# Half-slab weight loads in prompt attention, six gate buffers in the attention output product, and another staging order in the first down product

## The chip, the cores and the metric

The kernel runs on one core of one Trainium2 chip. The metric is the device time of one execution in microseconds (us); the time of a kernel is the median of several such runs. In the profile PE is the matrix engine (PEld its weight loads), DVE the vector engine, ACT the scalar engine, POOL the general engine, and SP the engine that here only issues transfers. "SPq" is SP's queue: it issues its DMAs in order, and a DMA that waits for a semaphore holds up those behind it.

## What is computed

One inference step of a decoder layer over 544 tokens (512 of a prompt, 32 of eight samples), float32, width 1024:

```python
mod = silu(c) @ w_ada + b_ada                      # six vectors of 1024
h   = rmsnorm(x, norm1) * (1 + sc1) + sh1
bg, cg, xin, q, k.., v.., gates, merge = split(h @ w_in)
y_a = (bg * conv3(cg * xin)) @ w_out_conv          # short convolution branch
o_b = sparse_attention(q, k.., v.., gates)         # compressed + selected + window
ga, gb = sigmoid(merge)
x   = x + g1 * ((ga * y_a + gb * (o_b @ w_o_nsa)) @ w_out)
h2  = rmsnorm(x, norm2) * (1 + sc2) + sh2
x   = x + g2 * ((silu(h2 @ w_gate) * (h2 @ w_up)) @ w_down)
y   = rmsnorm(x, norm_f)
```

For the prompt, every query attends in 128-query blocks; for the samples, past rows come from a paged cache.

## The kernel before, in words

Activations stand feature-major, 128 features by 544 tokens, in eight chunks. A product in full precision is made of three matrix passes over a high and a low part of both operands (`mm3`, L252 to L254). The weights are packed on the host into slabs `wt` of up to 128 x 2048 floats (8 KB a partition). `slab(...)` (L235) takes one of three rotating buffers `raw` (L216) and starts one load on SP (L238); `split(...)` (L241) turns 128 output columns of a slab into `wh` on ACT (L247) and `wl` on DVE (L248), each with two buffers. The framework traces the program, orders the instructions of each engine once, when it is built, by priority in program order and by its own estimate of when each is ready, and adds the waits. Within an engine that order is then fixed: an instruction that waits holds all that stand behind it. `issue_after` adds an ordering edge on one engine, not a wait.

Three places matter here.

**Prompt attention** (L1345 to L1560). Sixteen units, for g = 0..3 and i = 3..0; they are numbered 0 to 15 below. A unit (`unit`, L1434) makes scores on PE (`sp`, L1448 to L1456), takes their minimum with the distance table on DVE (L1461), exponentiates on ACT (L1462), and in its second half transposes the probabilities on PE (`ptp`, L1489), copies them on ACT or DVE (L1403, L1405) and multiplies by the values (`acc`, L1483). Beside each unit the loop does one step of `oc_gen` (L1383), which is half of one of eight chunks of the convolution branch's output product (eight triples of matrix passes over `yin`, then a DVE multiply by a reloaded gate `ga`, L1395), and one `mod_slab` (L426), which multiplies the conditioning vectors by one `ada` slab straight out of `raw` (`modp`, L432; 32 short matmuls). So 16 `ada` slabs and four `oc` slabs, each of 1 MB and each `oc` slab holding two chunks, pass through the three `raw` buffers, in order of the requests. An `ada` buffer comes free with its `modp`, an `oc` buffer with the split of its second chunk. `presum` (L562) adds a DRAM-to-DRAM copy (`pre`, L573, on SP) and an accumulating one (L576, on POOL) for later stages. In units 0, 1, 4, 5, 8 and 9 the loop also reloads the queries and keys of the next g (L1360, L1367).

**The attention's output product** (L1562 to L1600). Eight chunks with `o` slabs; each result is multiplied by the sigmoid of a reloaded gate `gb` (L1592, L1593; two buffers), added to the convolution branch's result and split again. Ahead of it the whole residual input `x1` (2.1 MB) is requested (L1565).

**The first down product** (`down_plain`, L1855), which stands between the gate product and the up product of the third pair of the feed-forward network. Eight chunks are staged in six places, two each in `U`, `Gs[1]` and `dsp`, from which POOL adds them to `x1` in DRAM by an accumulating DMA (L1853). Chunks 6 and 7 use the first two places again. After it the up product's first results are added into `U` (L1838).

Of the kernel before, what the change touches and what calls it, by code (L numbers as in the profile page):

```python
# [20 lines left out]
KC = 8  # L21
# [74 lines left out]
def _slabs():  # L96

    r = np.arange(1024).reshape(8, 128)
    d = {}

    def add(key, src, rows, c0, n):
        d[key] = (src, rows, np.arange(c0, c0 + n))

    for v in range(2):
        d["phi", v] = ("w_phi1", np.arange(2048).reshape(16, 128) + 2048 * v, np.arange(128))
    for s in range(24):
        add(("ada", s), "w_ada", r, s * 256, 256)
    add(("gate",), "w_in", r, C_GATE, 128)

    def quarters(key, src, cols, rows=r):  # L110
        n = len(rows)
        d[key] = (src, np.concatenate([rows[:n // 2], rows, rows[n // 2:]]), np.concatenate([np.tile(cols[i], (n // 2, 1)) for i in (1, 0, 0, 1)]))

    for ty in range(3):
        for v in range(2):
            quarters(("kv", ty, v), "w_in", [C_KV + ty * 512 + v * 256 + m * 128 + np.arange(128) for m in range(2)])
    for gp in range(2):
        for rp in range(2):
            quarters(("q", gp, rp), "w_in", [np.concatenate([np.arange(64) + C_Q + (2 * gp + gg) * 256 + (2 * rp + r2) * 64 for gg in range(2)]) for r2 in range(2)])
    for k2 in range(4):  # L120
        for n, c in (("cg", C_CG), ("xin", C_XIN), ("bg", C_BG), ("ga", C_MERGE), ("gb", C_MERGE + 1024)):
            if n == "ga" or (n == "gb" and k2 < GB7) or (n in ("cg", "xin", "bg") and k2 >= CV7):
                quarters((n, k2), "w_in", [c + k2 * 256 + m * 128 + np.arange(128) for m in range(2)])
            else:
                add((n, k2), "w_in", r, c + k2 * 256, 256)
        add(("oc", k2), "w_out_conv", r, k2 * 256, 256)
        p = np.arange(128)
        j = np.arange(8)
        rows = (2 * (j[:, None] // 4) + p[None, :] // 64) * 256 + (j[:, None] % 4) * 64 + p[None, :] % 64
        add(("o", k2), "w_o_nsa", rows, k2 * 256, 256)  # L130
        add(("out", k2), "w_out", r, k2 * 256, 256)
        for ph, (c0, n) in enumerate(PHASES):
            r6 = np.arange(c0 * 128, (c0 + n) * 128).reshape(n, 128)
            if ph in (1, 2):
                quarters(("dn", ph, k2), "w_down", [k2 * 256 + m * 128 + np.arange(128) for m in range(2)], np.concatenate([r6[0::2], r6[1::2]]))
            else:
                add(("dn", ph, k2), "w_down", r6, k2 * 256, 256)
    for c2 in range(FC // 2):
        for n, w in (("fg", "w_gate"), ("fu", "w_up")):
            if c2 == 0:  # L140
                add((n, c2), w, r, 0, 256)
            else:
                quarters((n, c2), w, [c2 * 256 + m * 128 + np.arange(128) for m in range(2)])
    return d
# [12 lines left out]
def build(tc, a, o):  # L157
# [16 lines left out]
    def lin_ps(nm):  # L174
        return ps.tile([128, 512], F32, tag="g", bufs=5, name=nm)

    def tp_ps(nm):
        return ps.tile([128, 512], F32, tag="g", bufs=5, name=nm)
# [9 lines left out]
    def nm(s):  # L188
        uid[0] += 1
        return f"{s}_{uid[0]}"  # L190
# [44 lines left out]
    def slab(*key):  # L235
        nk, ncol = len(SLABS[key][1]), SLABS[key][2].shape[-1]
        v = raw_tile("raw")[:, 0:nk * ncol]
        last_slab[0] = queue(lambda: sync.dma_start(v, a["wt"][SLAB_AT[key], :, 0:nk * ncol]))  # L238
        return v.rearrange("p (k f) -> p k f", k=nk)

    def split(view, nk=8, perm=None):  # L241
        wh = wpool.tile([128, 8, 128], F32R, tag="wh", bufs=2, name=nm("wh"))
        wl = wpool.tile([128, 8, 128], F32R, tag="wl", bufs=2, name=nm("wl"))
        oh, ol = wh[:, 0:nk, :], wl[:, 0:nk, :]
        if perm is not None:
            oh, ol = perm(oh), perm(ol)
        act.activation(oh, view, AF.Copy)  # L247
        dve.tensor_sub(ol, view, oh.bitcast(F32))  # L248
        return wh[:, 0:nk, :], wl[:, 0:nk, :]
# [158 lines left out]
    def hcols(hf):  # L408
        return slice(*HS[hf])
# [13 lines left out]
    MODS = {4: (0,), 5: (1,), 6: (2,), 7: (3,), 8: (4, 5), 9: (6, 7)}  # L423
    AHEAD = {4: 3, 5: 4, 6: 5, 7: 6, 8: 7}

    def mod_slab(s, v=None):  # L426
        v = slab("ada", s) if v is None else v
        p = tp_ps(nm("modp"))
        for k in range(KC):
            for hh in range(2):  # L430
                j = (k % 2) * 2 + hh
                pe.matmul(p[32 * j:32 * j + 32, 0:128], lhsT=cT[:, k, :], rhs=v[:, k, hh * 128:(hh + 1) * 128], start=(k < 2), stop=(k >= 6))  # L432
        m4 = wpool.tile([128, 128], F32, tag="m4", bufs=2, name=nm("m4"))
        act.activation(m4, p[:, 0:128], AF.Copy)
        if modp:
            modp.pop()()
        modp.append(lambda: mod_fin(s, m4))
# [929 lines left out]
            sync.dma_start(t[n * 64:n * 64 + 64].rearrange("p r x -> p (r x)").bitcast(F32), q_dr[gp][n][me])  # L1367
        return t

    oc_slabs = [slab("oc", 0)]  # L1370
    qst, kst = q_stack(0), k_stack(0)
    for br in range(2):
        vload = sync.dma_start(vtok[br].rearrange("p i f -> p (i f)"), v_dr[br])
    with tc.issue_after(vload.ins):
        mods_ahead = [slab("ada", 8), slab("ada", 9)]
    yst = ExitStack()
    y3p = mkpool(yst, "y3p", side="right")
    yh, yl = (y3p.tile([128, KC, NT], F32R, name="yin_" + n_) for n_ in ("hi", "lo"))
# [2 lines left out]
    pc0 = at.tile([128, 4, 4, 32], F32, name="pc0")  # L1381

    def oc_gen():  # L1383
        for k2 in range(4):
            so = slab("oc", k2) if k2 else oc_slabs[0]
            for kk in range(2):
                k = k2 * 2 + kk
                wh, wl = split(so[:, :, kk * 128:(kk + 1) * 128])
                for hf in range(2):
                    t = ga_next.pop(0) if ga_next else ga_tile(hf)  # L1390
                    sync.dma_start(t, ga_dr[k][:, hcols(hf)])
                    p = lin_ps(nm("lin"))[:, 0:HW[hf]]
                    for kc in range(KC):
                        mm3(p, wh, wl, yh[:, kc, hcols(hf)], yl[:, kc, hcols(hf)], kc, kc == 0, kc == KC - 1)
                    dve.tensor_mul(C[:, k, hcols(hf)], p, t)  # L1395
                    yield

    pcnt, p_ops, e_ops = [0], [], []

# [131 lines left out]
    for g in range(4):  # L1531
        qs, ks = qst, kst
        pc = cmp_probs(g, qs) if g else first_pc
        for i in (3, 2, 1, 0):
            u = unit(g, i, ks, qs, pc) if g or i < 3 else first_unit
            if g or i < 3:
                next(u)
            next(ocf, None)
            mod_slab(nslab, mods_ahead.pop(0) if mods_ahead else None)
            nslab += 1  # L1540
            presum(g > 0 or i < 2)
            if prev is not None:
                next(prev, None)
            prev = u
            if g < 3 and i == 3:
                qst = q_stack(g + 1)
            if g < 3 and i == 2:
                kst = k_stack(g + 1)
# [13 lines left out]
    x1_slot = lambda n, dt, w=NT: x1p.tile([128, KC * NT // w, w], dt, tag="x1", bufs=1, name=n)  # L1562
    x1 = x1_slot("x1", F32)
    lo_slot = lambda n, dt: x1p.tile([128, KC, NT], dt, tag="lo", bufs=1, name=n)
    sync.dma_start(x1.rearrange("p k n -> p (k n)"), a["xT"])  # L1565
    n2st = ExitStack()
    n2 = mkpool(n2st, "n2")
    zst = ExitStack()
# [15 lines left out]
    for k2 in range(4):  # L1584
        sy = slab("o", k2)
        win_shift(k2 // 2, k2 % 2)
        presum()
        for kk in range(2):
            k = k2 * 2 + kk
            cs = slice(kk * 128, kk * 128 + 128)  # L1590
            gb = op5.tile([128, NT], F32, tag="gb", bufs=2, name=nm("gb"))
            sync.dma_start(gb, gb_dr[k])  # L1592
            act.activation(gb, gb, AF.Sigmoid)  # L1593

            def ev(hf, p):
                c = hcols(hf)
                dve.tensor_mul(gb[:, c], p, gb[:, c])
                dve.tensor_add(C[:, k, c], C[:, k, c], gb[:, c])
                to_hilo(C[:, k, c], zh[:, k, c], zl[:, k, c])
            linear(split(sy[:, :, cs]), (oh, ol), ev)  # L1600
# [254 lines left out]
    def down_plain():  # L1855

        nk = PHASES[0][1]
        stg = [t[:, m, :] for t in (U, Gs[1], dsp) for m in range(2)]
        for m in range(KC):
            if m % 2 == 0:  # L1860
                sl_ = slab("dn", 0, m // 2)
            w = split(sl_[:, :, (m % 2) * 128:(m % 2) * 128 + 128], nk=nk)
            t = stg[m % 6]
            for hf in range(2):
                p = lin_ps(nm("dn"))[:, 0:HW[hf]]
                for k in range(nk):
                    mm3(p, w[0], w[1], fh[k][:, hcols(hf)], fl[k][:, hcols(hf)], k, k == 0, k == nk - 1)
                gated(t, hcols(hf), p, m, g2m)
            add_x1(m, t)
# [246 lines left out]
```

## Time and profile before

| | us |
|---|---|
| median of 3 runs (lowest, highest) | 1189.29 (1188.83, 1190.13) |
| profiled execution, its own time | 1192.38 |
| its span in the profile | 1190.6 |
| PE busy | 1174.8 |
| DVE busy | 850.7 |
| ACT busy | 639.8 |
| POOL busy | 106.8 |

Busy time of PE is modelled from pipelined matmuls, so 99% of the span says that PE seldom stands still, not that it runs at its peak. What can be gained by moving transfers shows as idle time of PE and as time at a lower granted clock; both are found in tables of stretches. A chain of waits tells which instruction released which; a row of it is start, duration, and engine with line or transfer. In rows of instructions, a bracket at the end gives the idle time of that engine just before it and what ended it.

### The profile page before, as it was taken

Reading aid. Unit: us, or ns where it says so; the run is one execution under the profiler, and the core shown is the slowest. Engines: PE = TensorE matmul, PEld = TensorE weight load, DVE = VectorE, ACT = ScalarE, POOL = GpSimd, SP = SyncE. Lnnn points to the kernel's source line nnn. Section 1 sums busy time; section 2 is a strip of 40 time slices with the busy share of each in tenths; the row PEclk is TensorE's granted clock in tenths of the full one; section 3 lists DMA queues with packets and bytes.
Section 4 is the critical chain, followed back from the end, with each engine's and each line's share of the span. In section 5 each row is a group of like instructions: output and inputs, shape, how many; then the busy total and the mean of one; then the engine's idle time right before and its main releaser. Section 6 shows DMA issues by size and latency. Waiting matters only on the chain.

```text
span 1190.6 us, 25817 instructions
## 1 busy us (share of the span) xinstructions
PE 1174.8 (99%) x10098; PEld 1090.9 (92%) x10098; DVE 850.7 (71%) x1930; ACT 639.8 (54%) x1302; POOL 106.8 (9%) x157
## 2 busy tenths in 40 slices
PE   9999999999999999999999999999999999999997
PEld 6999999999999888887776779999999999999996
DVE  2539986788774676777776866758847887887776
ACT  1416644565555333486665765527646566666542
POOL 1000340000000111020101100000010001001000
PEclk9999999999999999999999999999999999999999
DMA  9964765888666998979886878544356359349412
GB/s 339 357 254 143 195 203 159 266 255 231 216 182 216 360 371 316 306 209 245 243 224 183 216 222 286 173 164 165 91 153 197 129 136 238 128 123 222 173 54 75
DMA packets 87643, 250.68 MB, mean 211 GB/s; under 512 B 9560, under 2 KB 20184, under 8 KB 76010
## 3 DMA queue, kind: packets, MB, share of 16 engines
q1 hardware_dynamic: 73890, 223.56, 54.1%
q0 software_dynamic: 12912, 24.17, 12.7%
q8 instruction: 79, 1.29, 0.4%
q10 hardware_dynamic: 720, 1.31, 0.3%
q14 instruction: 42, 0.34, 0.1%
HBM read 217.64 MB, written 66.33 MB: 239 GB/s over the span
## 4 chain that ended last, share of the span: by engine, by line
PE 83%; DVE 5%; DMA 5%; issue 5%; ACT 1%; POOL 0%; ACTq 0%; SPq 0%; POOLq 0%; DVEq 0%
PE wA L254 8%; PE wA L252 7%; PE wA L253 7%; PE lin L252 6%; PE lin L253 6%; PE lin L254 6%; PE phi L677 5%; PE wC L253 4%; PE wC L254 4%; PE wC L252 4%; PE acc L1483 3%; PE ptp L1489 3%; PE modp L432 2%; PE wB L252 2%; PE wB L253 2%
## 5 line engine op out<-in xcount | busy, mean ns | idle before, releaser
L412 ACT ACTIVATE Wh<-raw 128x512 fp32r<-128x512 f32 (+3 forms) x83 | 63.1, 760 | 50.2 <-PE wA L253 34.5
L413 DVE TENSOR_TENSOR Wl<-raw,Wh 128x512 fp32r<-128x512 f32 (+3 forms) x83 | 70.9, 855 | 22.9 <-ACT Wh L412 22.4
L301 ACT ACTIVATE work<-wA 128x272 f32<-128x272 f32 x102 | 39.9, 391 | 68.9 <-PE wA L254 67.1
L1462 ACT ACTIVATE P<-P,nms 128x384 f32<-128x384 f32 (+3 forms) x120 | 64.9, 543 | 20.1 <-DVE nms L1461 19.4
L1461 DVE CUSTOM_DVE_ANT_0 P<-sp,ta 128x384 f32<-128x384 f32 (+3 forms) x120 | 52.1, 469 | 30.0 <-PE sp L1449 22.6
L413 DVE TENSOR_TENSOR wl<-ws,wh 128x1024 fp32r<-128x1024 f32 (+1 forms) x50 | 59.5, 1189 | 16.8 <-ACT wh L412 15.3
L412 ACT ACTIVATE wh<-ws 128x1024 fp32r<-128x1024 f32 (+1 forms) x50 | 51.3, 1026 | 35.0 <-PE wC L253 23.3
L413 DVE TENSOR_TENSOR wl<-raw,wh 128x1024 fp32r<-128x1024 f32 (+2 forms) x56 | 64.7, 1155 | 4.5 <-ACT wh L412 4.2
L252 PE MATMUL lin<-h_h,wh 128*128 128x288 f32 (+1 forms) x224 | 66.9, 299 | 0.3 <-ACT pts L197 0.3
L253 PE MATMUL lin<-h_l,wh 128*128 128x288 f32 (+1 forms) x224 | 64.6, 289 | 0.0
L254 PE MATMUL lin<-h_h,wl 128*128 128x288 f32 (+1 forms) x224 | 64.5, 288 | 0.0
L677 PE MATMUL phi<-gt,wphi 128*128 128x128 f32 x512 | 61.4, 277 | 0.7 <-DMA gt<-in_cache_cmp 0.7
L412 ACT ACTIVATE wh<-raw 128x1024 fp32r<-128x1024 f32 (+2 forms) x56 | 55.9, 999 | 11.3 <-PE wB L253 4.9
L677 PEld LDWEIGHTS phi<-gt,wphi 128*128 128x128 f32 x512 | 59.1, 192 | 2.9 <-DMA gt<-in_cache_cmp 1.7
L248 DVE TENSOR_TENSOR wl<-raw,wh 128x1024 fp32r<-128x1024 f32 (+1 forms) x42 | 47.1, 1121 | 20.1 <-ACT wh L247 19.8
L247 ACT ACTIVATE wh<-raw 128x1024 fp32r<-128x1024 f32 (+1 forms) x42 | 40.9, 973 | 35.6 <-PE lin L253 25.0
L576 POOL DMA_DIRECT2D pre<-in_wt x29 | 28.4, 980 | 340.6 <-DMA pre<-in_wt 340.4
L252 PE MATMUL wA<-S_hi,Wh 128*128 128x272 f32 x184 | 53.5, 291 | 0.0
L254 PE MATMUL wA<-S_hi,Wl 128*128 128x272 f32 x184 | 53.1, 290 | 0.2 <-DVE Wl L413 0.2
L253 PE MATMUL wA<-S_lo,Wh 128*128 128x272 f32 x184 | 53.1, 288 | 0.0
L252 PEld LDWEIGHTS lin<-h_h,wh 128*128 128x128 f32 x224 | 42.2, 188 | 10.9 <-issue 10.3
L668 DVE TENSOR_TENSOR xs<-gt 128x1024 f32<-128x1024 f32 x16 | 19.5, 1222 | 36.3 <-PE phi L677 20.6
(592 smaller groups left out, 4392.6 us busy)
## 6 DMA issues: line engine op xcount, KB each, us to landing
raw<-in_wt SPq DMA_DIRECT2D x67, 1024.0 KB, 5.6
raw<-in_wt SPq DMA_DIRECT2D x25, 768.0 KB, 5.0
sraw<-in_cache_sel SPq DMA_DIRECT2D x64, 256.0 KB, 5.1
gt<-in_cache_cmp SPq DMA_DIRECT2D x60, 256.0 KB, 5.5
pre<-in_wt SPq DMA_DIRECT2D x21, 512.0 KB, 9.1
pre<-in_wt POOLq DMA_DIRECT2D x21, 512.0 KB, 7.3
wraw<-in_cache_winT SPq DMA_DIRECT2D x8, 1024.0 KB, 8.4
raw<-pre SPq DMA_DIRECT2D x21, 256.0 KB, 5.6
```

Source lines behind the costliest of these rows:

```text
L247: act.activation(oh, view, AF.Copy)
L248: dve.tensor_sub(ol, view, oh.bitcast(F32))
L252: pe.matmul(p, lhsT=wh[:, k, :], rhs=xh, start=start, stop=False, **kw)
L253: pe.matmul(p, lhsT=wh[:, k, :], rhs=xl, start=False, stop=False, **kw)
L254: pe.matmul(p, lhsT=wl[:, k, :], rhs=xh, start=False, stop=stop, **kw)
L301: o_.snap_ops.append(act.activation(t, p, AF.Copy))
L412: act.activation(hi, src, AF.Copy)
L413: return dve.tensor_sub(lo, src, hi.bitcast(F32))
L677: pe.matmul(po[:, c0:c0 + 128], lhsT=w[:, ch], rhs=x[:, :, ch * 16:ch * 16 + 16], start=(n_ == 0 and ch == 0), stop=(n_ == 2 and ch == 7))
L1461: p_ops.append(dve.tensor_tensor_reduce(out=t[:, 0:n], in0=sps[br], in1=t_dist[:, 512 - n:512], scale=-hs, scalar=3e38, op0=ALU.add, op1=A ...
L1462: e_ops.append(act.activation(t[:, 0:n], t[:, 0:n], AF.Exp, scale=-1.0, bias=nms[:, c:c + 1], accum_out=sums[:, c:c + 1]))
L1483: pe.matmul(acc[br * 64:br * 64 + 64, :], lhsT=vtok[br][:, j, g * 64:(g + 1) * 64], rhs=pts_[br], start=(j == 0), stop=False)
```

## The change

The `oc` slabs are packed as eight slabs of one chunk each, 4 KB a partition. In prompt attention the three `raw` buffers are taken at once and cut into six halves of 4 KB. A list gives the loads in order of use: `oc` 0 and 1, the `ada` slabs 8 to 11 in two halves each, and then for k = 2 to 7 `oc` k and the `ada` slabs 8 + 2k and 9 + 2k, which are those of units 2k and 2k + 1. `prefetch` starts the next loads into whatever halves are free; it is called after each split of an `oc` chunk, which frees one half, and after each `mod_slab`, which frees two. The chunks of `oc` 0 and 1 go out ahead of the queries and keys, the `ada` slabs 8 and 9 after the values, as before. In the output product `gb` has six buffers, and `x1` is requested after the gate of chunk 3 and behind the newest slab's load. In the first down product the places are used in the order `dsp`, `U`, `Gs[1]`.

```diff
-        add(("oc", k2), "w_out_conv", r, k2 * 256, 256)
+        for k in (2 * k2, 2 * k2 + 1):
+            add(("oc", k), "w_out_conv", r, k * 128, 128)
...
-    def mod_slab(s, v=None):
-        v = slab("ada", s) if v is None else v
+    def mod_slab(s, v):
         p = tp_ps(nm("modp"))
+        v = v if callable(v) else (lambda k, v_=v: v_[:, k])
...
-    oc_slabs = [slab("oc", 0)]
+    halves = [t[:, 1024 * n:1024 * n + 1024] for t in [raw_tile("raw") for _ in range(3)] for n in range(2)]
+    loads = [("oc", 0), ("oc", 1), ("ada", 8), ("ada", 9), ("ada", 10), ("ada", 11)]
+    for k in range(2, KC):
+        loads += [("oc", k), ("ada", 8 + 2 * k), ("ada", 9 + 2 * k)]
+    loads = [(key, n) for key in loads for n in range(1 + (key[0] == "ada"))]
+    landed = {}
+
+    def prefetch():
+
+        while halves and loads:
+            key, n = loads.pop(0)
+            t = halves.pop(0)
+            last_slab[0] = sync.dma_start(t, a["wt"][SLAB_AT[key], :, 1024 * n:1024 * n + 1024])
+            landed.setdefault(key, []).append(t)
...
+    halves, later_halves = halves[0:2], halves[2:]
+    prefetch()
     qst, kst = q_stack(0), k_stack(0)
     for br in range(2):
         vload = sync.dma_start(vtok[br].rearrange("p i f -> p (i f)"), v_dr[br])
+    halves = later_halves
     with tc.issue_after(vload.ins):
-        mods_ahead = [slab("ada", 8), slab("ada", 9)]
+        prefetch()
...
-        for k2 in range(4):
-            so = slab("oc", k2) if k2 else oc_slabs[0]
-            for kk in range(2):
-                k = k2 * 2 + kk
-                wh, wl = split(so[:, :, kk * 128:(kk + 1) * 128])
...
+        for k in range(KC):
+            so = landed.pop(("oc", k))
+            wh, wl = split(so[0].rearrange("p (k f) -> p k f", k=8))
+            halves.extend(so)
+            prefetch()
...
-            mod_slab(nslab, mods_ahead.pop(0) if mods_ahead else None)
+            mod_slab(nslab, mod_views(nslab))
+            halves.extend(landed.pop(("ada", nslab)))
+            prefetch()
...
-    sync.dma_start(x1.rearrange("p k n -> p (k n)"), a["xT"])
...
-            gb = op5.tile([128, NT], F32, tag="gb", bufs=2, name=nm("gb"))
+            gb = op5.tile([128, NT], F32, tag="gb", bufs=6, name=nm("gb"))
             sync.dma_start(gb, gb_dr[k])
+            if k == 3:
+                with tc.issue_after(last_slab[0].ins):
+                    sync.dma_start(x1.rearrange("p k n -> p (k n)"), a["xT"])
...
-        stg = [t[:, m, :] for t in (U, Gs[1], dsp) for m in range(2)]
+        stg = [t[:, m, :] for t in (dsp, U, Gs[1]) for m in range(2)]
```

`mod_views` hands `mod_slab` the two halves of an `ada` slab. The arithmetic is the same.

More of the change, by code (lines that the diff above doesn't have):

```diff
@@ L431, in mod_slab @@
                 j = (k % 2) * 2 + hh
-                pe.matmul(p[32 * j:32 * j + 32, 0:128], lhsT=cT[:, k, :], rhs=v[:, k, hh * 128:(hh + 1) * 128], start=(k < 2), stop=(k >= 6))
+                pe.matmul(p[32 * j:32 * j + 32, 0:128], lhsT=cT[:, k, :], rhs=v(k)[:, hh * 128:(hh + 1) * 128], start=(k < 2), stop=(k >= 6))
         m4 = wpool.tile([128, 128], F32, tag="m4", bufs=2, name=nm("m4"))
@@ L1368, in q_stack, with mod_views @@
         return t
-    oc_slabs = [slab("oc", 0)]
+    halves = [t[:, 1024 * n:1024 * n + 1024] for t in [raw_tile("raw") for _ in range(3)] for n in range(2)]
[10 more added lines that the diff above has]
+            landed.setdefault(key, []).append(t)
+    def mod_views(s):
+        hs = [t.rearrange("p (k f) -> p k f", k=4) for t in landed[("ada", s)]]
+        return lambda k: hs[k // 4][:, k % 4]
+    halves, later_halves = halves[0:2], halves[2:]
+    prefetch()
     qst, kst = q_stack(0), k_stack(0)
@@ L1383, in oc_gen @@
     def oc_gen():
-        for k2 in range(4):
-            so = slab("oc", k2) if k2 else oc_slabs[0]
-            for kk in range(2):
-                k = k2 * 2 + kk
-                wh, wl = split(so[:, :, kk * 128:(kk + 1) * 128])
[L1389 to L1396, printed above, removed]
+        for k in range(KC):
[3 more added lines that the diff above has]
+            prefetch()
+            for hf in range(2):
+                t = ga_next.pop(0) if ga_next else ga_tile(hf)
+                sync.dma_start(t, ga_dr[k][:, hcols(hf)])
+                p = lin_ps(nm("lin"))[:, 0:HW[hf]]
+                for kc in range(KC):
+                    mm3(p, wh, wl, yh[:, kc, hcols(hf)], yl[:, kc, hcols(hf)], kc, kc == 0, kc == KC - 1)
+                dve.tensor_mul(C[:, k, hcols(hf)], p, t)
+                yield
     pcnt, p_ops, e_ops = [0], [], []
```

## The prediction

> **What bounds the kernel now.** I read the page first, for the engine that carries the span.
>
> ```profile
> span 1190.6 us, 25817 instructions
> PE 1174.8 (99%) x10098; PEld 1090.9 (92%) x10098; DVE 850.7 (71%) x1930; ACT 639.8 (54%) x1302; POOL 106.8 (9%) x157
> PE 83%; DVE 5%; DMA 5%; issue 5%; ACT 1%; POOL 0%; ACTq 0%; SPq 0%; POOLq 0%; DVEq 0%
> ```
>
> PE is busy for 1174.8 of 1190.6 us. The change alters no matmul, so all it can win is PE's idle time and time at a lower clock. To find these I went through the span in stretches of 1 us and kept those in which PE was idle or its clock low; the table of stretches then gives their prices. After the length, the first figure of a row is PE's busy time; the last three are granted clock, DMA share and GB/s.
>
> ```profile
> 640.00:642.00 2.00, 0.20 (x2) 0.01 (x1) 2.00 (x7) 0.43 (x2) 0.00 (x0) 1.00 0.13 22
> 643.10:646.60 3.50, 3.50 (x41) 2.72 (x40) 2.50 (x13) 1.77 (x8) 0.00 (x0) 0.51 0.14 40
> 718.00:736.00 18.00, 18.00 (x142) 17.72 (x142) 10.47 (x21) 9.57 (x16) 0.89 (x1) 1.00 0.91 305
> 736.00:738.00 2.00, 1.53 (x13) 1.31 (x12) 1.85 (x4) 0.69 (x3) 0.00 (x0) 1.00 0.48 171
> 904.00:906.00 2.00, 1.54 (x12) 1.32 (x11) 1.97 (x3) 0.00 (x0) 0.00 (x0) 1.00 0.24 77
> 920.00:922.00 2.00, 1.65 (x13) 1.43 (x13) 2.00 (x3) 1.65 (x4) 0.00 (x0) 1.00 0.18 67
> ```
>
> One hole in prompt attention (1.80 us idle, then 3.5 us at clock 0.51, which costs 3.5 x 0.49 = 1.72), one in the attention's output product (0.47), two in the feed-forward network (0.46 and 0.35). Each of the three edits touches one of these places. Together they hold 4.80 us, 0.40% of the median. About 0.2% (2.4 us) is what a measurement of this kernel can tell from no change.
>
> **Part 1, the half slabs.** The chain of waits shows what made the hole at 640:
>
> ```profile
> 627.07 1.00 PE modp L432 x30
> ...
> 628.46 9.80 DMA raw<-in_wt
> ...
> 638.28 1.07 ACT wh L247
> ...
> 639.38 1.23 DVE wl L248
> ...
> 671.27 1.01 PE modp L432 x32
> ```
>
> The waits of PE in this stage name what it stood for:
>
> ```profile
> PE sp L1448 <- DVE nms L1461: 1.8, 1, 1.8
> ```
>
> The load that starts at 628.46 takes the buffer that unit 9's `modp` (627.07) has just freed. It brings the slab of `oc` chunks 6 and 7. Chunk 6 belongs to unit 12, whose `modp` runs at 671, so PE wants it some 30 us later. But its split stands far earlier in the fixed orders of ACT and DVE, as soon as the build thought the data there. The load took 9.80 us, ACT and DVE waited for it in line, and behind them stood the minima (`nms`), which free the PSUM that PE's scores need. So PE paid for a transfer that it did not yet need. The other three chunks that were split right after their slab's load (2, 4 and the first `o` chunk) show no ACT wait (no bracket), this one 2.08 us:
>
> ```profile
> 541.05 1.06 ACT L247 ACTIVATE wh<-raw 128x1024 fp32r<-128x1024 f32 x1
> 584.84 1.05 ACT L247 ACTIVATE wh<-raw 128x1024 fp32r<-128x1024 f32 x1
> 638.28 1.06 ACT L247 ACTIVATE wh<-raw 128x1024 fp32r<-128x1024 f32 x1 [2.08 <-DMA raw<-in_wt]
> 687.69 1.05 ACT L247 ACTIVATE wh<-raw 128x1024 fp32r<-128x1024 f32 x1
> ```
>
> Why was it late? Ahead of it two 1 MB slabs went out together, one held back until an `oc` buffer was free:
>
> ```profile
> 618.96 0.38 SPq L238 DMA_DIRECT2D raw<-in_wt  x1
> ...
> 620.10 0.63 SPq L238 DMA_DIRECT2D raw<-in_wt  x1
> ```
>
> After the change an `oc` half is free with its own split, not with the second chunk's, so no `ada` slab is held back: units with an even number release 1.5 MB in three halves, those with an odd number 1 MB. Walking the list of halves through the sixteen units gives: `oc` k goes out after `modp` of unit 2k - 3 and behind one `ada` half; every `ada` half goes out more than one unit ahead. Chunk 6 thus still starts at about 628.5, but behind a burst that is spread out. Its landing:
>
> ```profile
> raw<-in_wt SPq DMA_DIRECT2D x67, 1024.0 KB, 5.6
> raw<-in_wt SPq DMA_DIRECT2D x4, 512.0 KB, 3.6
> kl<-k_dr1l SPq DMA_DIRECT2D x4, 256.0 KB, 12.6
> x<-in_xT SPq DMA_DIRECT2D x1, 2176.0 KB, 13.2
> ```
>
> One `ada` half and one `oc` half are 1 MB together: 5.6 us by the median, so 634 instead of 638.26, before ACT reaches the split at 636.2 (638.28 less 2.08). The hole and the low clock after it go: 3.52 us. What is next in line there is the otmp copy and the minima, which then run 2 us earlier than PE asks.
>
> What it adds: 20 DMA issues at 0.38 us, 8 us of SP over 220 us, beside everything. And six newly loaded chunks (2 to 7) whose splits follow a landing, where before there were three; chunks 3, 5 and 7 formerly found their half landed. Two of them start among the queries and keys:
>
> ```profile
> 548.30 0.54 SPq L1367 DMA_DIRECT2D qs<-q_dr1h  x1
> 548.90 0.93 SPq L1367 DMA_DIRECT2D qs<-q_dr1l  x1
> ...
> 550.55 0.51 SPq L238 DMA_DIRECT2D raw<-in_wt  x1
> ...
> 552.73 2.07 SPq L1360 DMA_DIRECT2D kl<-k_dr1l  x2
> ```
>
> The same happens after 600 for unit 7. There a transfer takes up to 12.6 us (the `kl` row). Bounds for a split that comes too early: 0 if the fixed order allows for the queue, as it did in three of the four rows above; 12.6 - 7.7 = 4.9 us of ACT wait if the order is set as for chunk 6 (636.2 less 628.46 is 7.7 us after the issue). I take one quarter of the 1.80 us that one of four cost, 0.45, for each of the two, so +0.90 us; the rows above are of the same instruction, the bound of another transfer.
>
> The Trainium skill has a rule against this edit (Perfetto Trace Analysis, section DMA Optimizations): larger transfers use the memory better, and small ones should be batched. The two `raw` rows agree in direction, as two 512 KB loads one after the other would take 7.2 us against 5.6. By the rule each of the six chunks would land 1.6 us later, and if PE paid for all of it the sum would be worse by 9.6 us and the kernel slower; this works the same way as rival (c), which has its price from rows alone.
>
> Also moved: the first `o` slab. The first `raw` buffer is now whole again only after unit 14, not 13:
>
> ```profile
> 680.57 0.99 PE modp L432 x26
> 696.20 1.01 PE modp L432 x32
> 707.96 1.01 PE modp L432 x32
> ```
>
> So it starts at about 697, the next two at 709. With 5.6 us, or even 13.2 as `x1`, it lands at 703 to 710, and PE starts on it at 718: free.
>
> **Part 2, six gate buffers and the later x1.**
>
> ```profile
> 715.10 0.33 SPq L1565
> ...
> 716.54 15.98 DMA gb<-gb_dr
> ...
> 733.11 1.04 ACT wh L247
> ...
> 736.01 1.15 DVE wl L248
> ```
>
> SP waits to send `x1` (2.1 MB, 13.2 us), the gates queue behind it, the second lands at 732.5, ACT runs its sigmoid and only then the split of the third chunk, and PE idles 0.47 us. Afterwards the gates have no `x1` ahead of them; 272 KB each, six at once are 1.6 MB, under the 13.2 us of `x1`, so the second is there before 725. Gain 0.47, at worst 0. `x1` itself is passed by gates and an `o` slab; it is first used when this product is done, eight chunks at 18.0/142 x 48 = 6.1 us after 718, or 767, so it has 30 us of cover. What is late next is the `o` slabs, started at 709 for use from 730: covered.
>
> **Part 3, the staging order.**
>
> ```profile
> 886.32 0.86 POOL L1853 DMA_DIRECT2D x_dr<-work  x1 [2.15 <-ACT work L1847]
> ...
> 895.76 0.86 POOL L1853 DMA_DIRECT2D x_dr<-work  x1 [2.57 <-ACT work L1847]
> ...
> 903.17 0.44 DVE L1838 TENSOR_TENSOR work<-wB,work 128x272 f32<-128x272 f32 x1 [2.41 <-DMA x_dr<-work]
> ```
>
> The up product's first sum into `U` waits until chunk 6 has left `U` by the DMA of 895.76, which lands some 7.3 us later, just before DVE starts at 903.17. DVE idles 2.41 us, the splits queue behind it, and PE has its holes at 904 and 920. With the new order chunks 6 and 7 leave from `dsp`, and `U` last holds chunk 3, sent at 886.32; at the same 7.3 us it is free at 893.6, 9 us before it is wanted. `dsp` was last used by the gates of the first chunks, and is next written by a later down product. Gain 0.81; at least 0.46 if the second hole is DVE's own.
>
> **The sum.** 3.52 + 0.47 + 0.81 = 4.80, less 0.90: 3.9 us. Against the profiled execution (1192.38 us, of which 1.78 lie outside its span) that is 1188.5, with a span of 1186.7. The median of the runs is 3.09 us lower than the profiled time; I take the same difference from it: 1185.4.
>
> **Rivals.** (a) *The clock does not fall in the timed runs of before.* Then there is 1.72 less to win: 1187.1. For it: the hole is only 1.80 us and the timed runs are 3.09 us shorter than the profiled one. Against it: the three lie within 1.3 us of each other. By the Trainium skill (TensorE: Matmul & The Clock Gate, section What's actually happening) the clock halves after an idle window of about 3.4 us that runs free of the kernel. This trace disagrees on the length of the idling, 1.80 us, and agrees on that of the low clock, 3.5. By the rule as it stands nothing was lost to the clock.
>
> (b) *The wait moves.* One of the six splits stands too early as chunk 6 did, hole and clock again cost 3.52, and parts 2 and 3 alone remain: 1189.29 - 1.28 = 1188.0. For it: one of four did so. That the halves should wait for whole buffers, and nothing come earlier, gives the same.
>
> (c) *Slower: chunks 3 and 5 behind the queries and keys.* ACT waits 4.9 us at each, PE 0.3 less (it lost 1.80 of 2.08), and the clock takes 1.72 each time: 2 x 6.3 = 12.6 us, so 1189.29 - 4.80 + 12.6 = 1197.1; with one of them 1190.8. It decides when the split's place in ACT's order is under 12.6 us from the issue. Against it: at 541 and 584 the order was late enough. For it: before, no split ever followed a load among these.
>
> **How the numbers follow.** Forecast 0.57, (a) 0.13, (b) 0.16, (c) 0.14. Faster than 1186.9: the forecast and a third of (a), 0.61. Same: the rest of (a), (b) and a little of (c), 0.27. Slower: 0.12. The forecast's own range goes from 4.80 and the runs' spread of 1.3 us, 1183.2, to 1186.9; to leave out no more than 2 in 10 the range goes up to one wait of (c), 1190.8.
>
> **What would show it.** Right: no idle PE at 640 and granted clock 1.00 through prompt attention; no DMA wait before any split there; gates' sigmoids before 725 and no hole at 736; the sum into `U` released by PE, not by a DMA; no hole near 904 and 920. Wrong: a bracket `<-DMA raw` before one of the splits of chunks 2 to 7 with idle PE some 4 us on, above all after 550 and 603, or a new stretch at half clock anywhere.

## The result and the profile after

The changed kernel takes 1200.49 us (median of 6 runs, 1197.61 to 1203.43) beside 1190.16 us of the kernel before (6 runs, 1188.83 to 1191.64): ratio 1.0086, 95% interval 1.0066 to 1.0105. It is slower by 0.9%; the forecast, 1185.4 in a range up to 1190.8, had the wrong sign. The profiled execution took 1202.13 us. The page of the changed kernel:

```profile
span 1200.1 us, 25844 instructions
PE 1178.7 (98%) x10098; PEld 1093.2 (91%) x10098; DVE 852.8 (71%) x1930; ACT 639.9 (53%) x1302; POOL 109.0 (9%) x157
```

The matmuls are the same in number (10098), and the span is 9.5 us longer. PE's busy time grew by 3.9 us and its idle time by 5.6 us. The lines stand further down in the changed code: L247 is now L248, L1448 is L1470. The table of stretches of the changed kernel, for every place where PE stood still in the changed stages and for the two places of part 3 (columns as in the prediction: PE's busy time behind the length, granted clock third from the end):

```profile
531.00:533.00 2.00, 1.81 (x10) 0.47 (x9) 1.04 (x1) 1.91 (x3) 0.00 (x0) 1.00 1.04 234
565.00:567.00 2.00, 1.09 (x27) 0.66 (x19) 1.45 (x5) 2.00 (x7) 0.00 (x0) 1.00 1.00 203
585.00:587.00 2.00, 1.53 (x9) 0.75 (x8) 1.02 (x1) 2.00 (x4) 0.55 (x1) 1.00 0.19 64
638.50:642.00 3.50, 1.21 (x8) 0.67 (x7) 1.21 (x2) 2.30 (x4) 0.71 (x1) 0.95 0.32 119
642.00:645.40 3.40, 3.40 (x15) 1.62 (x12) 1.99 (x10) 1.31 (x5) 0.17 (x1) 0.54 0.73 130
668.50:671.00 2.50, 1.60 (x8) 0.99 (x8) 1.77 (x4) 1.94 (x3) 0.47 (x1) 1.00 0.28 104
711.00:717.00 6.00, 1.29 (x11) 1.12 (x10) 3.02 (x11) 2.94 (x9) 0.54 (x1) 0.98 0.46 160
717.00:720.40 3.40, 3.40 (x30) 3.16 (x33) 1.31 (x10) 2.69 (x12) 0.33 (x1) 0.53 0.71 94
726.00:731.00 5.00, 4.36 (x30) 3.06 (x29) 2.70 (x6) 4.14 (x10) 0.10 (x1) 1.00 1.02 286
904.00:906.00 2.00, 2.00 (x18) 2.00 (x18) 0.19 (x1) 1.18 (x2) 0.33 (x1) 1.00 1.08 331
920.00:922.00 2.00, 2.00 (x18) 2.00 (x17) 2.00 (x4) 1.49 (x3) 0.00 (x0) 1.00 0.03 8
```

Read it in three groups. From 531 to 671 PE idles 0.19 + 0.91 + 0.47 + 2.29 + 0.90 = 4.76 us and runs 3.40 us at clock 0.54 (3.40 x 0.46 = 1.56): 6.3 us where the kernel before lost 3.5. At 711 it idles 4.71 us and then runs 3.40 us at 0.53 (1.60): another 6.3 us, where the kernel before had no hole. At 904 and 920 it no longer stands still. The 0.64 at 726 is old: it is the wait for a copy that cost 0.69 at 715 to 718 before. The new losses, with this 0.64, are 13.3 us; the old ones are the prediction's 4.80 and the 0.69, so these places explain 7.8 of the 9.5 us. Another 0.7 us arose ahead of prompt attention: in the chain of waits the first `cpt` products stand at 496.93 before and at 497.62 after. The last 1.0 us stands in no hole of its own. It must be in PE's busy time, of which the low clock explains only 1.4 of the 3.9 us (1.56 + 1.60 after, 1.72 before).

Setting the same matmuls of the two profiles side by side tells more than adding up idle time. Those of the changed kernel start 0.7 us later in unit 0, 5.9 in unit 14, 11.9 in unit 15, 11.1 behind the gates and 9.8 behind the staging. So the stage of the chunks lost 5.3 us net, where idle time and clock account for 2.8 (6.3 less 3.5); the gates won 0.8 and the staging 1.4, where idle time alone says 0.5 and 0.8. Part of the price of a hole thus stands in PE's busy time.

What stands ahead of the holes shows in ACT's instructions at the split (the bracket is ACT's idle time before it, and what ended it), for chunks 2 to 7 and the first `o` chunk:

```profile
530.88 1.06 ACT L248 ACTIVATE wh<-raw 128x1024 fp32r<-128x1024 f32 x1 [0.89 <-DMA raw<-in_wt]
561.82 1.06 ACT L248 ACTIVATE wh<-raw 128x1024 fp32r<-128x1024 f32 x1 [2.62 <-DMA raw<-in_wt]
584.89 1.06 ACT L248 ACTIVATE wh<-raw 128x1024 fp32r<-128x1024 f32 x1 [3.61 <-DMA raw<-in_wt]
616.14 1.06 ACT L248 ACTIVATE wh<-raw 128x1024 fp32r<-128x1024 f32 x1 [1.64 <-DMA raw<-in_wt]
639.70 1.06 ACT L248 ACTIVATE wh<-raw 128x1024 fp32r<-128x1024 f32 x1 [3.88 <-DMA raw<-in_wt]
669.03 1.06 ACT L248 ACTIVATE wh<-raw 128x1024 fp32r<-128x1024 f32 x1 [1.06 <-DMA raw<-in_wt]
712.61 1.06 ACT L248 ACTIVATE wh<-raw 128x1024 fp32r<-128x1024 f32 x1 [4.54 <-DMA raw<-in_wt]
```

All seven waited for a load, where before one of four did. The chain of waits names four of these loads and how long they were under way; the waits of PE name the instructions behind the splits:

```profile
551.60 10.19 DMA raw<-in_wt
...
631.16 8.52 DMA raw<-in_wt
...
663.10 5.91 DMA raw<-in_wt
...
702.80 9.79 DMA raw<-in_wt
```

```profile
PE sp L1470 <- DVE nms L1483: 4.7, 1, 4.7
PE acc L1505 <- ACT PT L1425: 3.5, 4, 2.3
PE cps L1437 <- ACT cpT L1434: 1.2, 2, 0.9
PE ptp L1511 <- DVE nms L1483: 0.9, 1, 0.9
```

PE does not wait for `wh` or `wl`. It waits for copies and minima of attention that stand in line behind the split. At the largest place DVE did nothing at all for 7.67 us, because its half of the split waited for ACT's half, and with it the minima behind:

```profile
713.70 1.23 DVE L249 TENSOR_TENSOR wl<-raw,wh 128x1024 fp32r<-128x1024 f32 x1 [7.67 <-ACT wh L248]
714.85 0.28 DVE L1483 CUSTOM_DVE_ANT_0 P<-sp,ta 128x128 f32<-128x128 f32 x1
```

### The profile page after: what moved, and what is told of

The parts are those of the page before. It is cut to its first block, busy times and chain, and to the rows that moved or that the text cites. A ratio compares the mean times of both kernels' runs of the same rounds, so it can differ in the third digit from the quotient of the medians.

```text
span 1200.1 us, 25844 instructions
## 1 busy us (share of the span) xinstructions
PE 1178.7 (98%) x10098; PEld 1093.2 (91%) x10098; DVE 852.8 (71%) x1930; ACT 639.9 (53%) x1302; POOL 109.0 (9%) x157
## 3 DMA queue, kind: packets, MB, share of 16 engines
q0 software_dynamic: 12912, 24.17, 12.6%
## 4 chain that ended last, share of the span: by engine, by line
PE 88%; DVE 4%; DMA 3%; issue 2%; ACT 1%; SPq 0%; POOL 0%; POOLq 0%; DVEq 0%; ACTq 0%
PE wA L255 8%; PE wA L253 8%; PE wA L254 8%; PE phi L678 7%; PE lin L253 6%; PE lin L254 6%; PE lin L255 6%; PE wC L254 4%; PE wC L255 4%; PE wC L253 4%; DMA raw<-in_wt 3%; PE acc L1505 3%; PE ptp L1511 2%; PE modp L433 2%; PE wB L253 2%; PE wB L254 2%
## 5 line engine op out<-in xcount | busy, mean ns | idle before, releaser
L248 ACT ACTIVATE wh<-raw 128x1024 fp32r<-128x1024 f32 (+1 forms) x42 | 41.0, 976 | 55.3 <-PE lin L254 28.1
L1505 PE MATMUL acc<-PT,vtok 128*64 128x512 f32 x160 | 47.5, 633 | 3.5 <-ACT PT L1425 3.5
```

The lines of the kernel that those rows point to most:

```text
L1505: pe.matmul(acc[br * 64:br * 64 + 64, :], lhsT=vtok[br][:, j, g * 64:(g + 1) * 64], rhs=pts_[br], start=(j == 0), stop=False)
```

## The experiments

Two theories. **Early splits**: the split of each newly loaded slab stands in the fixed order of ACT and DVE near the moment at which the build expects the load, long before PE needs the chunk; the load is later, and attention's own work waits behind it. **Contention**: forty half loads in place of twenty whole ones make the transfers as such slower, and PE starves of weights wherever the splits stand. The shared runs of the kernel before had a median of 1190.26 us beside the first four kernels, 1189.92 beside the next four and 1190.00 beside the last two.

**Which part is it?** The half slabs alone (gates, `x1` and staging as before):

```diff
+    sync.dma_start(x1.rearrange("p k n -> p (k n)"), a["xT"])
...
-            gb = op5.tile([128, NT], F32, tag="gb", bufs=6, name=nm("gb"))
+            gb = op5.tile([128, NT], F32, tag="gb", bufs=2, name=nm("gb"))
...
-        stg = [t[:, m, :] for t in (dsp, U, Gs[1]) for m in range(2)]
+        stg = [t[:, m, :] for t in (U, Gs[1], dsp) for m in range(2)]
```

> The half slabs alone, with the gates, x1 and the staging as before. Two theories stand against each other for the 10 us lost. Early splits: the build put the split of every newly loaded oc chunk, and of the first o chunk, into the orders of ACT and DVE at the time at which it thought the load landed; each stands before its real landing and PE pays. Contention: 40 loads of 512 KB instead of 20 of 1 MB make all transfers of this stage slower. By both this kernel has the whole loss and none of the small gains: 1201 us, with holes of PE near 566, 586, 640, 670 and 712, and the two at 905 and 921 as before. If it is near 1190, the loss comes from the gates and x1.

Measured: 1199.82 us (4 runs, 1198.82 to 1202.77), ratio 1.0082 (1.0051 to 1.0113). The whole loss is in the half slabs. The splits of chunks 2 to 7 and of the first `o` chunk waited for loads here too, between 0.17 and 3.71 us. The stretches around the `o` split of this kernel:

```profile
708.00:712.60 4.60, 0.71 (x7) 0.54 (x6) 2.60 (x9) 2.30 (x5) 0.00 (x0) 0.96 0.77 240
712.60:716.10 3.50, 3.50 (x17) 3.40 (x17) 1.25 (x12) 2.85 (x14) 0.87 (x1) 0.56 0.24 22
```

The other half of the change, the gates with the later `x1` and the staging, on the kernel before:

```diff
-    sync.dma_start(x1.rearrange("p k n -> p (k n)"), a["xT"])
...
-            gb = op5.tile([128, NT], F32, tag="gb", bufs=2, name=nm("gb"))
+            gb = op5.tile([128, NT], F32, tag="gb", bufs=6, name=nm("gb"))
...
-        stg = [t[:, m, :] for t in (U, Gs[1], dsp) for m in range(2)]
+        stg = [t[:, m, :] for t in (dsp, U, Gs[1]) for m in range(2)]
```

> The six gate buffers with the later x1 and the staging order alone, half slabs left out. By the steps of the prediction, on which both theories agree: 0.47 + 0.81 less, 1189 us, no holes of PE near 737, 905 and 921, the hole at 640 with its low clock as before. If the later x1 or the gates were at fault, slower than 1192.

Measured: 1188.70 us (10 runs, 1187.61 to 1190.20), ratio 0.9983 (0.9973 to 0.9993). Parts 2 and 3 bring 1.6 us, where 1.28 was forecast. In its profile the hole at 640 is still there, 1.58 us long, but the clock does not fall after it:

```profile
640.00:642.00 2.00, 0.42 (x4) 0.22 (x3) 2.00 (x9) 0.59 (x3) 0.00 (x0) 1.00 0.12 19
642.00:646.00 4.00, 4.00 (x55) 3.55 (x56) 3.07 (x15) 3.37 (x14) 0.00 (x0) 1.00 0.27 57
```

**Is it where the splits stand?** The changed kernel, every load as it was, with the split of a chunk ordered behind the exponentials and minima of the unit before the one that uses it. No load is edited, only the place of two instructions; a few copies and minima beside them change places as well, and since a half comes free with its split, some later loads go out a few us later (the one at 533.22 goes out at 538.96).

```diff
+        done = None
         for k in range(KC):
             so = landed.pop(("oc", k))
-            wh, wl = split(so[0].rearrange("p (k f) -> p k f", k=8))
+            with tc.issue_after(done[0].ins) if done else ExitStack(), tc.issue_after(done[1].ins) if done else ExitStack():
+                wh, wl = split(so[0].rearrange("p (k f) -> p k f", k=8))
...
                 dve.tensor_mul(C[:, k, hcols(hf)], p, t)
+                done = p_ops[-1], e_ops[-1]
                 yield
```

> The changed kernel with one thing more: the split of an oc chunk k is ordered on ACT and on DVE behind the exponentials and minima of unit 2k - 1. Loads, halves and their sizes stay. Early splits: the DMA waits before the splits of chunks 2 to 7 go, and with them PE's holes near 566, 586, 634, 640 (with half clock) and 670, together 6.4 us; the wait before the first o chunk stays: 1194 us. Contention: the loads are as late as ever and ACT waits just as long at the new place, or PE waits for wh in units 6, 10 and 12: 1200 us.

Measured: 1193.41 us (10 runs, 1188.01 to 1194.49), ratio 1.0012 (0.9992 to 1.0031). None of the chunks' splits waits for a load any more, and the hole at 640 is gone. The `o` split, which this edit does not touch, still waited 4.49 us, and what is left of the loss in this profile is there:

```profile
639.00:642.00 3.00, 3.00 (x23) 2.91 (x22) 2.52 (x13) 2.52 (x10) 0.00 (x0) 1.00 0.77 124
702.50:708.00 5.50, 0.84 (x6) 0.67 (x6) 2.83 (x10) 2.52 (x6) 0.00 (x0) 0.98 0.70 187
707.90:711.30 3.40, 3.40 (x17) 3.40 (x17) 1.13 (x10) 2.68 (x14) 0.87 (x1) 0.51 0.38 37
```

**Can the `o` slab come in time?** As before, and the half that chunk 6 leaves is not handed to the next load, so that the buffer for the `o` slab should be whole earlier:

```diff
-            halves.extend(so)
+            if k != 6:
+                halves.extend(so)
             prefetch()
```

> The same with the half that chunk 6 leaves not given back, so that the last ada slabs use the other two buffers, and the first raw buffer is whole after the split of chunk 7: the first o slab can start near 670 instead of 703. Early splits: the hole near 712 (4.7 us, and 1.7 for the clock) goes as well: 1187.5 us, faster than before by the three holes of before. Contention: no gain over the kernel with the ties alone.

Measured: 1193.15 us (10 runs, 1191.97 to 1194.30), ratio 1.0024 (1.0011 to 1.0037): a miss. The slab went out at 686.42, 8 us earlier than in the tied kernel (694.14), and not near 670, as I had counted on, since the tied split of chunk 7 (683.10) now frees its buffer late. Its split moved forward as well, and again stood ahead of the landing; PE waited 3.5 us for a copy behind it (`m`, that of a `modp`):

```profile
697.04 1.06 ACT L248 ACTIVATE wh<-raw 128x1024 fp32r<-128x1024 f32 x1 [4.46 <-DMA raw<-in_wt]
```

```profile
PE ptp L1515 <- ACT m L435: 3.5, 1, 3.5
```

The 8 us won on the load bought nothing. This speaks against lateness of the load as the thing to mend, and for the place of the split.

**Then the place of the `o` split alone must do it.** The tied kernel, with the first `o` split also behind the last unit's minima and exponentials:

```diff
-            linear(split(sy[:, :, cs]), (oh, ol), ev)
+            with tc.issue_after(p_ops[-1].ins) if k == 0 else ExitStack(), tc.issue_after(e_ops[-1].ins) if k == 0 else ExitStack():
+                w_ = split(sy[:, :, cs])
+            linear(w_, (oh, ol), ev)
```

> The changed kernel with the splits of out-convolution chunks tied as in e3 and with the first output slab's first split also tied, on both engines, behind the minima and exponentials of the last attention unit. In e3 that split stood at 704.0 us ahead of the last unit's minima, waited 4.49 us for its slab, and PE lost 4.66 us idle plus 3.4 us at half clock (1.7 us). Early splits: no DMA wait in front of that split, no hole near 704, 6.4 us below e3: 1187.0 us, span about 1185.4, so 0.2 to 0.35% below before. Contention (halves as such make loads slow and PE starve): the slab lands no earlier, the wait only moves to PE's first matmul of the output product at 721, and the time stays within 1 us of e3, 1192 to 1194 us.

Measured: 1188.08 us (12 runs, 1187.09 to 1189.05), ratio 0.9984 (0.9976 to 0.9993). Expected were 1187.0 and a span of 1185.4; the span is 1185.5, and the median 1.1 us above. From prompt attention to the output product the order of ACT's instructions is that of the tied kernel but for the place of this one split; on DVE, its half has changed places with minima of the last unit. The `o` split, the waits of PE and the stretches:

```profile
705.22 1.04 ACT L248 ACTIVATE wh<-raw 128x1024 fp32r<-128x1024 f32 x1
```

```profile
PE acc L1508 <- ACT PT L1428: 0.6, 1, 0.6
PE pt L1225 <- DVE S L1216: 0.3, 1, 0.3
PE cps L1440 <- ACT cpT L1437: 0.3, 1, 0.3
```

```profile
565.00:567.00 2.00, 2.00 (x15) 1.90 (x16) 1.33 (x8) 1.98 (x7) 0.82 (x1) 1.00 1.10 195
639.00:642.00 3.00, 3.00 (x24) 2.91 (x23) 2.15 (x11) 2.67 (x11) 0.24 (x1) 1.00 0.72 100
702.50:708.00 5.50, 5.50 (x71) 5.01 (x69) 4.26 (x26) 5.10 (x18) 0.00 (x0) 1.00 0.83 202
```

The split has no bracket, PE is busy for 5.50 of 5.50 us where it had 0.84, and no wait of PE is longer than 0.6 us. Contention, which had the time stay within 1 us of the tied kernel, is out as the cause of the loss: the loads are the same forty halves, and the median to landing of 512 KB loads is 6.9 us in this kernel and 6.8 in the changed one.

The reverse, the `o` split tied and the chunks left as the change has them (the last diff on the changed kernel):

> The changed kernel with only the first output slab's first split tied behind the last unit's minima and exponentials; the chunk splits stay where the change put them. If the two groups of holes add up, this wins about what e10 wins over e3, 6.4 us: 1200.5 - 6.4 = 1194.1 us, with the chunk holes at 566, 586, 640 and 670 unchanged and the one at 712 to 716 gone. If the delay of the chunks only hands the hole on (the slab is issued late because the chunks are), PE waits at its first matmul of the output product instead and the time stays at 1198 us or more.

Measured: 1197.27 us (6 runs, 1194.47 to 1200.88), ratio 1.0063 (1.0045 to 1.0081), between the two expectations. Its profiled execution, 1194.47, is the shortest of the six: the place at 711 is mended, those of the chunks stay, with other lengths.

```profile
639.00:641.00 2.00, 0.90 (x4) 0.38 (x4) 1.32 (x2) 2.00 (x4) 0.84 (x1) 1.00 0.04 13
666.00:669.00 3.00, 1.30 (x7) 0.75 (x6) 1.48 (x3) 1.85 (x3) 0.35 (x1) 1.00 0.18 66
711.00:717.00 6.00, 5.95 (x67) 4.45 (x67) 5.03 (x18) 5.06 (x14) 0.87 (x1) 1.00 0.79 255
```

The profile is 7.7 us shorter than that of the changed kernel (1202.13): the 6.3 us at 711, and 1.6 for the clock, which does not fall here. So far the two groups add up. By the medians, though, this edit won 3.2 us and not 6.4. The mean clock is 0.998 in the profile and 0.995 to 0.998 in the five longer executions. Where the other 3.2 us went is open.

**Are half slabs worth anything once the splits are tied?** The kernel before with whole slabs, the same tie, six gate buffers and the other staging order, that is the edits of the second and third experiment together on the kernel before:

> The kernel before, whole 8 KB slabs, with the chunk splits tied as in e3, six gate buffers and the other staging order: no half slab. e2 (without the tie) came at 1188.7 us with a hole of 1.57 us at 640 and no fall of the clock. If the tie takes that hole away: 1187.0 us, and if the clock fell in most timed runs of e2 as it did in the profile of before, 1186.2. If half slabs bring something of their own (buffers free earlier), e10 is below this by more than 0.5 us; if they bring nothing once splits are tied, the two agree within 1.2 us. Early splits says they agree.

Measured: 1187.35 us (12 runs, 1187.06 to 1188.23), ratio 0.9976 (0.9967 to 0.9984), the lowest median of all kernels here, and below both the kernel before and the changed one. The span of its profile is the same as with the halves, 1185.5 us, and PE is busy throughout at the old holes of prompt attention and of the staging:

```profile
639.00:642.00 3.00, 3.00 (x24) 2.91 (x23) 2.17 (x11) 2.67 (x11) 0.18 (x1) 1.00 0.82 156
902.00:920.00 18.00, 18.00 (x146) 18.00 (x145) 17.06 (x30) 11.78 (x20) 0.00 (x0) 1.00 0.38 136
```

Halves gain nothing over whole slabs. The interval overlaps that of the tied halves, so a loss by them is not shown either.

**What is each of the other parts worth?** With the splits tied on the kernel before, alone, with the staging, and with the gates; the tie, beside the edits shown above, is this:

```diff
-                wh, wl = split(so[:, :, kk * 128:(kk + 1) * 128])
+                with tc.issue_after(done[0].ins) if done else ExitStack(), tc.issue_after(done[1].ins) if done else ExitStack():
+                    wh, wl = split(so[:, :, kk * 128:(kk + 1) * 128])
...
                     dve.tensor_mul(C[:, k, hcols(hf)], p, t)
+                    done = p_ops[-1], e_ops[-1]
                     yield
```

> The kernel before with only the chunk splits tied: no half slabs, no gate buffers, old staging order. Its profile's hole at 640 (1.80 us idle and 1.72 us of half clock) should go, the holes at 736, 904 and 920 stay. 1190.2 - 3.5 = 1186.7 us if the clock falls in timed runs as in the profile, 1188.4 us if it does not. If the hole at 640 was not caused by the place of the split, the time stays at 1190 us.

> The kernel before with the chunk splits tied and the other staging order, but two gate buffers as before. The profile of the tied kernel before (1189.04 us) has 1.09 us idle at 735 in front of the second gate's chunk and 0.37 us idle at 918 at the staging; the one with both parts beside the tie came at 1187.35 us. The staging alone should take the hole at 918 away and leave the one at 735: 1189.04 - 0.37 = 1188.7 us, up to 0.8 us less than the tie alone if holes at 904 and 920 both cost in timed runs as in the profile of before. If the staging brings nothing, 1189.0 us.

> The kernel before with the chunk splits tied and six gate buffers with the later load of x, but the old staging order. The hole of 1.09 us at 735 should go and the one of 0.37 us near 918 stay: 1189.04 - 1.09 = 1187.9 us. The two parts' gains, counted from the tie alone, should add up to the 1.7 us between 1189.04 and 1187.35 us, with the larger share here. If six buffers bring nothing, 1189.0 us with a wait for a gate still at 735.

Measured: 1189.04 us (ratio 0.9992, 0.9982 to 1.0002), 1187.87 (0.9977, 0.9966 to 0.9988) and 1188.50 (0.9983, 0.9972 to 0.9994), 12 runs each. So the tie alone won 0.9 us, with an interval that includes none, and not 1.8 or 3.5: the hole at 640 is gone in its profile, but that at the gates, 0.47 us before, is 1.1 there, the first of these rows. The staging adds 1.2 us and the gates 0.5, together 1.7, as the kernel with both had it; I had expected the larger share from the gates, and at most 0.8 from the staging. With the gates in, the one wait left of this kind is the staging's, the second row (the first from the tie alone, the second from the tie with gates):

```profile
PE lin L254 <- DVE wl L248: 1.1, 1, 1.1
```

```profile
PE wA L254 <- DVE Wl L413: 0.3, 1, 0.3
```

The intervals of the three overlap, so their order among themselves is not shown. In the profile of the one with the staging the gates caused no wait at all, but the first `o` split, which this edit does not tie, waited for its whole slab and PE lost 0.9 us behind it:

```profile
694.19 1.06 ACT L247 ACTIVATE wh<-raw 128x1024 fp32r<-128x1024 f32 x1 [1.86 <-DMA raw<-in_wt]
```

In the profiles of the other three kernels with whole slabs and tied chunks this split waited 0.42, 0.42 and 0.58 us, in that of the kernel before not at all. So whole slabs are not safe from this either.

## Why the prediction was wrong

**The hole at 640 goes.** It did not. The step that failed is "one `ada` half and one `oc` half are 1 MB together: 5.6 us by the median, so 634". Chunk 6's load went out at 631.16 and took 8.52 us to 639.68, and ACT waited 3.88 us where it had waited 2.08. I had taken a median over the whole kernel, which rests on the 12 landings recorded of 67 loads, for a load that had just taken 9.80 us in this very place. On the size of transfers the medians decide nothing: 512 KB loads have 6.8 us in the changed kernel and whole 1 MB loads 5.6 in the kernel before, but 7.9 in the one with tied whole slabs, the gates and the staging. Whether the Trainium skill's rule that I had cited (Perfetto Trace Analysis, section DMA Optimizations) holds for these halves, no run here shows. The time was not lost by it, as the tied kernels show.

**"I take one quarter of the 1.80 us that one of four cost, 0.45, for each of the two."** This is the step that cost the forecast its sign, together with the next. I took the three splits without a bracket as proof that "the fixed order allows for the queue". The place of a split is no fixed thing that a load meets or misses with some chance. It moves with the change: in the changed kernel ACT reached every one of the six between 4.4 and 7.8 us after the issue of its load, and then waited. The four whose landing is recorded start within 0.03 us of it. The bound of 4.9 us that I had worked out as the bad end was the right kind of number for all six (0.89 to 3.88 us measured), not for two with one chance in four. (The 12.6 us in it are no upper end, as I had read them: the `kl` row rests on one recorded landing of four, and one of the `kh` loads took 13.8.) By idle time and clock the places of the chunks cost 6.3 us in place of the 0.90 charged, and the 3.52 to be won were not won. That the build puts the split where it expects the load is argued from these places; the runs show only the place and what it costs.

**"It lands at 703 to 710, and PE starts on it at 718: free."** The load behaved about as I had it: issued behind unit 14's `modp`, landed at 712.59, and PE uses the chunk after its last attention work. It was not free, since I asked when PE needs the data and not what stands behind the split on ACT and DVE. It is the same trap that I had described for chunk 6 in the paragraph before, and I did not put the same question to this split. 6.3 us, more than all the gains forecast.

**Part 2** held in size only roughly: the wait at 736 is gone. The sigmoids did not come before 725 in the changed kernel (735.23, as SP itself ran late: the gates went out from 722.67 on). In the two kernels with the gates and no long hole in attention they did (721.26 with whole slabs, 723.29 with halves and every split tied); with only the chunks tied they came at 726.84. **Part 3** held as worked out: no hole at 904 or 920, and 1.2 us of time where 0.81 was forecast; the 1.4 by the starts of matmuls speak for the larger size.

**The rivals.** (c) had the right mechanism and sign and the nearest time, 1197.1, at wrong places: chunk 3 waited 2.62 us and chunk 5 1.64, neither the 4.9; chunks 4 and 6 and the `o` slab waited longer. So the nearness of its number is in part luck. Its condition, "among the queries and keys", was too narrow. (b), one of six too early, was the same idea at a sixth of its size. (a), that the clock does not fall in the timed runs of before, held for most of them as far as mean clocks tell: the profiles here with a fall ahead of their last 15 us have a mean of 0.997 at most, and 52 of the 77 shared runs of the kernel before have 0.998. So most of the 1.72 us charged to the clock were not there to win in the medians. This fits the kernel with every split tied, which won 1.8 us and not the 3.9 forecast, and the tie alone, which removed the hole at 640 and won 0.9 while the one at the gates grew by 0.6.

## What to carry to other kernels

An instruction that consumes a load stalls its whole engine where it stands in that engine's order, not where its result is needed: for each load that a change starts later, or newly, look up the instruction that reads it, what stands behind it, and who waits for that. If data is needed late, tie its first reader late; smaller loads and an earlier load did not help here while the reader moved forward with them. And when one of four such readers waits in the trace of before, ask for its mechanism and apply it to every reader that the change makes; don't take it as a chance of one in four.

## What the runs showed of the hardware

A short idle stretch of PE is enough to lower its clock. It fell to about half for some 3.4 us, within 1.2 us of the end of idle stretches of 1.80 us (before), 2.29 and 4.71 us (after), 3.89 us (half slabs alone), 4.66 us (chunks tied) and 3.54 us (the `o` slab earlier), and did not after 1.58 us (gates and staging) and 1.70 us (666 to 669 with only the `o` split tied). Whether one length between 1.70 and 1.80 us parts the two, or the moment matters too, these eight stretches do not show. The Trainium skill (TensorE: Matmul & The Clock Gate, section What's actually happening) tells of a window of about 3.4 us that runs free of the kernel; the length of the low stretch agrees with it, and the shortest idling that lowered the clock here is about half of that.

Executions of one kernel can differ by a whole hole. With only the chunks tied, three of the ten runs took 1188.0 to 1188.7 us at a mean clock of 0.998, and seven took 1192.3 to 1194.5 us at 0.995 or 0.996. The groups lie some 5 us apart, and one low stretch costs only 1.7 us (half of 3.4), so the clock alone does not explain it. The three take what the kernel with the `o` split tied as well takes (1187.1 to 1189.0 us), as if the `o` slab had come in time in them; no profile of one of the three shows it. The two kernels with no hole above 0.6 us from prompt attention on, tied halves and tied whole slabs, stay within 2.0 and 1.2 us over 12 runs each, and the kernel before, with its holes, spreads over 5.1 us in 29 runs beside them.
